# A streaming hybrid encoder step on one core: other bank counts, another pool order and a moved first-row block around the running streams' attention

## The chip, the cores and the metric

The kernel runs on one core of a Trainium2 chip. The core has a matrix engine (TensorE, PE in the profile, with its weight loads shown apart as PEld), a vector engine (DVE), a scalar engine (ACT), GpSimd (POOL) and a queue engine (SP) that issues nearly all transfers; 16 DMA engines carry them between the large memory (HBM) and the on-chip memory (SBUF). Matrix products land in PSUM, which has eight banks of 512 numbers of 32 bits for each of 128 partitions. The metric is the time of one launch in microseconds of device time; lower is better.

## The reference, cut to what matters

One layer of an encoder runs for two groups: one new stream of 1024 frames behind 16 meta rows (1040 rows) and eight running streams of 16 new frames each, with 272 cached rows of keys and values. Each row goes through a norm and one wide projection into queries, keys, values, the inputs of a state space scan and two gates. Attention (16 heads of 64) and the scan (32 heads of 64) run side by side and are merged through the gates; a causal convolution feed-forward net follows.

The attention is a stick-breaking one, with no softmax:

```python
def stick_breaking(q, k, v, q_pos, k_pos):
    z = jnp.einsum('bqhd,bshd->bhqs', q, k).astype(jnp.float32) * (SB_HEAD_DIM ** -0.5)
    reach = k_pos[None, :] < q_pos[:, None]
    log_beta = jax.nn.log_sigmoid(z)
    log_keep = jnp.where(reach, jax.nn.log_sigmoid(-z), 0.0)
    later = lax.cumsum(log_keep, axis=3, reverse=True) - log_keep
    w = jnp.where(reach, jnp.exp(log_beta + later), 0.0)
    return jnp.einsum('bhqs,bshd->bqhd', w.astype(v.dtype), v)
```

The kernel computes it without logarithms: beta = sigmoid(z), keep = 1 - beta, a running product of keep from the right, and weight = beta times the running product one place further right. In the merge the scan's output, normed over each of four groups, goes through `w_br_ssd` and is multiplied by its gate.

## The kernel before, in words

All 1168 rows (1040 + 128) are kept transposed in SBUF as `u`, split into a high and a low part, so that a 32-bit product is three matmuls in the faster form: high by high, high by low, low by high (`mm3`, lines 115, 118, 119). A projection block is 128 output columns: one weight load, split on ACT and DVE (lines 104 to 106), and three tiles of 384 to 400 rows, each 24 matmuls; 72 matmuls for a block.

The stages, in order: the norm; the scan (`phase_ssd`); the new stream's attention (`phase_att`); the running streams' attention (`phase_smp`); the merge (`phase_merge`); the feed-forward net (`phase_ffn`). Queries, keys and values go out to HBM (`s_qh`, `s_ql`, `s_kh`, `s_kl`, `s_v`) and are read back.

**The new stream's attention** goes over 8 pairs of heads. `head` (L684) loads KH, KL and QS (two buffers each), makes scores (L713, L716, PSUM tag `z`, two banks) for eight groups of 128 queries, each followed by `stick` (sigmoid on ACT, mask and complement on POOL, scan and product on DVE) into `beta0` to `beta7`, then transposes the weights (PSUM tag `wT`, two banks) and multiplies them by the values (PSUM tag `o`, two banks; L737, L738, L745). The groups begin at row 16; the first two query rows that are needed (rows 14 and 15) are done apart by `first_queries` (L752).

**The running streams' attention** (`sample_att`, L796) goes over 8 streams and 2 halves of the heads: 16 passes. Before them it loads the queries (`qhs`, `qls`), the new keys (`kxh`, `kxl`, 16 loads) and the last 16 cached key rows (`last`, 16 loads) and transposes these (PSUM tag `pk`). In a pass, 256 cached key rows are loaded (`ck`), transposed in two groups through `pk` and split into `Ksh` and `Ksl` (ACT copy, DVE subtraction); the queries are laid out on a diagonal (`qdh`, `qdl`, POOL); twelve matmuls make the scores (L873, L876, L877); sigmoid, mask, complement, scan and products give the weights; three transposes (`wT`) and a split follow; nine matmuls make the value product (L896 to L898, tag `o`); its result is copied to `od`, transposed back (`wT` again) and copied into `aout`, which is stored once at the end (L910).

**Filler.** Both stages alternate products with long chains on the other engines, so independent projection blocks are put between: 18 blocks of queries, keys and values and 16 gate blocks (`gate`, L659). `paced` (L960) draws a block when `done < len(marks) * rate` and ties each of its three tiles behind a marked matmul (`issue_after`): it may not be issued before it.

```python
    def paced(self, marks, done, rate):
        while self.fill and done < len(marks) * rate:
            at = lambda t: marks[min(int(t / rate), len(marks) - 1)]
            self.fill.pop(0)([at(done + t) for t in range(3)])
            done += 3
```

The new stream's attention has 64 marks and a rate of 1.17 and draws 25 of the 34 blocks. Of the other nine, `RESERVE` = 3 are held back for the start of the merge, and six go into the running streams' stage, at a rate of 3 x 6/16 tiles a pass; the mark of a pass is its first score matmul (L873).

**The merge.** `ssd_operands` (L925) makes 16 operands for `br_ssd`: for each it loads a block of the scan's output (`yt`, L933, two buffers), multiplies it by the row factors `rB` (L935, DVE), writes the high part (L936, ACT) and the low part (L937, DVE). The row factors come from `norm_rows` (L914) through HBM (`s_rs`). The second eight operands go into the slots of `u`. The held-back gate blocks stand ahead of `br_ssd` on PE.

**What sets the order.** Engines run their instructions in order, each with its own queue; SP issues the transfers in order too. A planner orders the instructions of each engine when the kernel is built, by estimated times, with earlier lines of the program first where two are ready. Each stage's pools are opened on top of the same base and closed again, so the next stage's tiles lie over the last stage's; a tile waits for the release of exactly those tiles that lay in its place. So the order in which a stage's pools are opened decides which old tile a new one has to wait for. The same holds for PSUM banks, in the order in which the tags are first used.

## Time and profile before

| what | us |
|---|---|
| median of 3 runs | 3043.59 (3042.37 to 3043.84) |
| profiled execution, its own time | 3041.27 |
| its span, first to last instruction | 3038.4 |
| PE busy in the span | 2936.0 |
| DVE, ACT, POOL busy | 1797.7, 1169.5, 600.3 |

The profiled execution is one run beside the three that were timed. The span leaves out some 2.9 us around the instructions. Shares of busy time are means over stages; the prediction reads the stages one by one. In the list of waits a line says who waited, for whom, how many us in total, how often, and the longest. In the list of instructions the bracket gives the idle time of the engine before the instruction and what ended it.

### The profile page before, as it was taken

The page shows a single profiled execution, that of the slowest core. Times are in us where ns is not written, and L with a number is a line of the kernel's source. Part 1 is how long each engine was busy: PE and PEld are TensorE (multiplying, and loading weights), DVE is VectorE, ACT ScalarE, POOL GpSimd, SP SyncE. Part 2 cuts the span into 40 slices and gives each one's busy share as a digit, 9 for nine tenths or more (in the row PEclk, how much of TensorE's full clock was granted, in tenths as well). Part 3 has the DMA queues.
Part 4 walks back from the last instruction along what each step waited for, and adds up shares of the span by engine and source line. Part 5 has one row for each costly group of instructions (what it writes and reads, how often), then busy time and mean ns, then how long its engine had stood idle before and what let it go on. Part 6 is the DMA issues. An engine that isn't in the chain of part 4 may idle for free.

```text
span 3038.4 us, 45425 instructions
## 1 busy us (share of the span) xinstructions
PE 2936.0 (97%) x17349; PEld 2792.5 (92%) x17349; DVE 1797.7 (59%) x2945; ACT 1169.5 (38%) x2294; POOL 600.3 (20%) x967
## 2 busy tenths in 40 slices
PE   7999999999999999999899899999999999999998
PEld 6998988979889999999799899999999999999997
DVE  6568677676666777777634441345755454545447
ACT  6432423324234554544444320214534242424245
POOL 0023132131232333333324000002201010101014
PEclk9999999999999999999899999999999999999999
DMA  5435355253474555544444553546211111111113
GB/s 187 110 95 150 97 141 151 76 157 104 133 215 130 165 153 143 155 124 110 84 122 149 158 180 97 149 109 190 73 46 44 43 44 43 43 43 38 41 43 118
DMA packets 445495, 338.43 MB, mean 111 GB/s; under 512 B 43991, under 2 KB 421155, under 8 KB 445279
## 3 DMA queue, kind: packets, MB, share of 16 engines
q1 hardware_dynamic: 445279, 335.54, 38.8%
q8 instruction: 136, 2.23, 0.3%
q14 instruction: 80, 0.66, 0.1%
HBM read 244.31 MB, written 91.15 MB: 110 GB/s over the span
## 4 chain that ended last, share of the span: by engine, by line
PE 43%; DVE 3%; DMA 2%; issue 1%; ACT 1%; POOL 0%; POOLq 0%; SPq 0%; ACTq 0%; DVEq 0%
PE mm L115 14%; PE mm L118 13%; PE mm L119 13%; DMA yt<-s_y 1%; DVE h L1192 1%; DVE sl L937 0%; DVE yt L935 0%; DVE wl L106 0%; PE o L896 0%; DMA ck<-in_cache_k 0%; PE tp L135 0%; PE o L898 0%; PE o L897 0%; DVE h L1170 0%; PE wT L135 0%
## 5 line engine op out<-in xcount | busy, mean ns | idle before, releaser
L115 PE MATMUL mm<-sh,wh 128*128 128x384 f32 (+3 forms) x2520 | 874.2, 347 | 13.3 <-ACT sh L936 5.1
L118 PE MATMUL mm<-sl,wh 128*128 128x384 f32 (+3 forms) x2520 | 870.5, 346 | 2.2 <-DVE sl L937 1.6
L119 PE MATMUL mm<-sh,wl 128*128 128x384 f32 (+3 forms) x2520 | 867.7, 345 | 0.0
L115 PEld LDWEIGHTS mm<-sh,wh 128*128 128x128 f32 (+1 forms) x2520 | 476.2, 189 | 28.0 <-issue 6.3
L118 PEld LDWEIGHTS mm<-sl,wh 128*128 128x128 f32 (+1 forms) x2520 | 476.6, 189 | 15.2 <-issue 9.2
L119 PEld LDWEIGHTS mm<-sh,wl 128*128 128x128 f32 (+1 forms) x2520 | 476.8, 189 | 8.9 <-issue 7.0
L115 PE MATMUL mm<-ph,wh 128*128 128x386 f32 x1248 | 424.3, 340 | 2.7 <-ACT ph L97 2.0
L118 PE MATMUL mm<-pl,wh 128*128 128x386 f32 x1248 | 424.7, 340 | 0.0
L119 PE MATMUL mm<-ph,wl 128*128 128x386 f32 x1248 | 422.4, 339 | 0.1
L106 DVE TENSOR_TENSOR wl<-wf,wh 128x1024 fp32r<-128x1024 f32 (+2 forms) x205 | 252.7, 1233 | 284.3 <-ACT wh L105 283.7
L105 ACT CAST wh<-wf 128x1024 fp32r<-128x1024 f32 (+2 forms) x205 | 212.5, 1037 | 485.1 <-PE mm L118 455.1
L1145 DVE SCALAR_TENSOR_TENSOR acc<-fx,cwf,acc 128x256 f32<-128x256 f32 (+1 forms) x352 | 170.8, 516 | 154.0 <-ACT acc L1143 150.1
L115 PEld LDWEIGHTS mm<-ph,wh 128*128 128x128 f32 x1248 | 236.2, 189 | 3.9 <-ACT ph L97 2.3
L119 PEld LDWEIGHTS mm<-ph,wl 128*128 128x128 f32 x1248 | 236.2, 189 | 0.9 <-DVE wl L106 0.5
L118 PEld LDWEIGHTS mm<-pl,wh 128*128 128x128 f32 x1248 | 235.2, 188 | 1.8
L680 DVE TENSOR_TENSOR_SCAN keep<-keep 128x144 f32<-128x144 f32 (+7 forms) x128 | 179.9, 1408 | 57.9 <-POOL keep L679 57.3
L115 PE MATMUL mm<-ah,wh 128*128 128x384 f32 x528 | 179.8, 340 | 0.0
L119 PE MATMUL mm<-ah,wl 128*128 128x384 f32 x528 | 179.2, 339 | 0.0
L118 PE MATMUL mm<-al,wh 128*128 128x384 f32 x528 | 178.6, 338 | 0.0
L1072 POOL TENSOR_TENSOR sq<-sq,sq 128x386 f32<-128x386 f32 (+1 forms) x42 | 60.2, 1433 | 467.1 <-ACT sq L1071 455.6
L98 DVE TENSOR_TENSOR wTl<-wT,wTh 128x512 fp32r<-128x512 f32 (+3 forms) x176 | 103.0, 602 | 80.6 <-ACT wTh L97 79.7
L1170 DVE TENSOR_TENSOR h<-mm,h 128x384 f32<-128x384 f32 x144 | 79.7, 555 | 119.8 <-PE mm L119 119.5
(326 smaller groups left out, 4535.2 us busy)
## 6 DMA issues: line engine op xcount, KB each, us to landing
wf<-in_w_in SPq DMA_DIRECT2D x80, 512.0 KB
wf<-in_w_up SPq DMA_DIRECT2D x44, 512.0 KB
t<-s_ac SPq DMA_DIRECT2D x36, 512.0 KB
wf<-in_w_down SPq DMA_DIRECT2D x28, 512.0 KB
wf<-in_w_out SPq DMA_DIRECT2D x24, 512.0 KB
s_y<-x SPq DMA_DIRECT2D x16, 577.0 KB
yt<-s_y SPq DMA_DIRECT2D x16, 577.0 KB
KH<-s_kh SPq DMA_DIRECT2D x32, 260.0 KB
```

The source lines that it names most:

```text
L98: nc.vector.tensor_tensor(out=l, in0=x, in1=h.bitcast(F32), op=ALU.subtract)
L105: nc.scalar.copy(wh, wf)
L106: nc.vector.tensor_tensor(out=wl, in0=wf, in1=wh.bitcast(F32), op=ALU.subtract)
L115: i = nc.tensor.matmul(p, wh[:, k, :], mh[:, c:c + w], start=s, stop=False)
L118: nc.tensor.matmul(p, wh[:, k, :], ml[:, c:c + w], start=False, stop=False)
L119: nc.tensor.matmul(p, wl[:, k, :], mh[:, c:c + w], start=False, stop=e)
L680: nc.vector.tensor_tensor_scan(out=K[:, ::-1], data0=K[:, ::-1], data1=K[:, ::-1], initial=1.0, op0=ALU.mult, op1=ALU.min)
L1072: nc.gpsimd.tensor_tensor(out=acc[:, :w], in0=acc[:, :w], in1=sq, op=ALU.add)
L1145: nc.vector.scalar_tensor_tensor(out=op, in0=src(q), scalar=w(q), in1=op, op0=ALU.mult, op1=ALU.add)
L1170: self.nc.vector.tensor_tensor(out=h, in0=p, in1=h, op=ALU.add)
L1192: nc.vector.tensor_scalar(out=h, in0=h, scalar1=self.gv[:, 24 + m:25 + m], scalar2=None, op0=ALU.mult)
```

## The change

- `first_queries` is called in the new stream's attention, ahead of the second head of the last pair, instead of at the start of the running streams' stage. Its tiles take the tags QS, KH and KL there, and its PSUM tiles that stage's `z` and `o`.
- In the running streams' stage `pk` has one bank instead of two and `o` two instead of one.
- The mark of a pass is its first value product (L896) instead of its first score matmul.
- `RESERVE` is 2 instead of 3: seven blocks go into the stage and two into the merge.
- The pools of both attention stages are opened in another order, and the fill stores' pool of the running streams' stage is opened last instead of first.
- `norm_rows` is called ahead of `sample_att` instead of behind it.

```diff
-RESERVE = 3
+RESERVE = 2
...
     def first_queries(self):
-        x = self.tile(ap, [128, 4, 288], F32R, 'Ksh').bitcast(F32).rearrange("p a b -> p (a b)")[:, :288]
+        x = self.tile(ap, [128, TP - T0], F32R, 'QS').bitcast(F32)[:, :288]
...
-        v = self.tile(ap, [128, 2, 512], F32R, 'Vsh').bitcast(F32)[:16].rearrange("p a (j c) -> p (a j) c", c=128)
+        v = self.tile(ap, [128, TP], F32R, 'KH').bitcast(F32)[:16, :1024].rearrange("p (j c) -> p j c", c=128)
...
-        Q = self.tile(ap, [128, 512], F32, 'last', bufs=2)[:, :256].rearrange("p (j c) -> p j c", c=32)
+        Q = self.tile(ap, [128, TP], F32R, 'KL').bitcast(F32)[:, :256].rearrange("p (j c) -> p j c", c=32)
...
-        ps = self.tile(pa, [128, 512], F32, 'z')
+        ps = self.tile(pa, [128, 512], F32, 'z', bufs=2)
...
-        po = self.tile(pa, [128, 512], F32, 'o')
+        po = self.tile(pa, [128, 512], F32, 'o', bufs=2)
...
     def sample_att(self, rate):
-            pk = self.tile(pa, [128, 512], F32, 'pk', bufs=2)
+            pk = self.tile(pa, [128, 512], F32, 'pk')
...
-                    pk = self.tile(pa, [128, 512], F32, 'pk', bufs=2)
+                    pk = self.tile(pa, [128, 512], F32, 'pk')
...
-                    mk = nc.tensor.matmul(z, qh, Kh[:, j], start=(j == 0), stop=False)
-                    if j == 0:
-                        marks.append(mk)
+                    nc.tensor.matmul(z, qh, Kh[:, j], start=(j == 0), stop=False)
...
-                po = self.tile(pa, [128, 512], F32, 'o')
+                po = self.tile(pa, [128, 512], F32, 'o', bufs=2)
...
-                    nc.tensor.matmul(po, wh[:, i], vh, start=(i == 0), stop=False)
+                    mk = nc.tensor.matmul(po, wh[:, i], vh, start=(i == 0), stop=False)
+                    if i == 0:
+                        marks.append(mk)
...
     def phase_att(self, right, rx):
-                'wTh', 'wTl', 'wf32', 'att', 'vf', 'KH', 'KL', 'QS', 'VV', 'keep', *(f'beta{i}' for i in range(8)))}
+                'KH', 'KL', 'QS', 'vf', 'keep', *(f'beta{i}' for i in range(8)), 'VV', 'wTh', 'wTl', 'wf32', 'att', 'fb', 'fw', 'fo')}
...
                 for e in range(2):
+                    if p == 7 and e == 1:
+                        self.first_queries()
                     marks += self.head(2 * p + e, v[:, :, 64 * e:64 * e + 64])
...
     def phase_smp(self):
-            mp = self.stp = self.pool(c2, "mixst", 3)
...
-                'aout', 'od', 'wTh', 'wTl', 'keep', 'beta', 'v', 'r', 'newton', 'qdh0', 'qhs', 'qls', 'kxh', 'kxl',
-                'last', 'V3h', 'V3l', 'qdl0', 'qdh1', 'qdl1', 'Ksh', 'Ksl', 'Vsh', 'Vsl',
-                'w30', 'w31', 'fb', 'fw', 'fo')}
+                'last', 'qhs', 'qls', 'kxh', 'kxl', 'qdh0', 'qdl0', 'qdh1', 'qdl1', 'Ksh', 'Ksl', 'V3h', 'V3l', 'v', 'r', 'newton',
+                'beta', 'keep', 'Vsh', 'Vsl', 'w30', 'w31', 'wTh', 'wTl', 'od', 'aout')}
+            self.stp = self.pool(c2, "mixst", 3)
...
-            self.first_queries()
+            self.norm_rows(self.ap)
             self.sample_att(3 * len(self.fill) / 16)
-            self.norm_rows(self.ap)
```

## The prediction, made before the changed kernel was run

> **What bounds the kernel now.** I read the page's shares first, then busy time by stretch from the last head's tail to the gated branch, then TensorE's (PE) waits in those stretches, then single instructions.
>
> ```profile
> PE 2936.0 (97%) x17349; PEld 2792.5 (92%) x17349; DVE 1797.7 (59%) x2945; ACT 1169.5 (38%) x2294; POOL 600.3 (20%) x967
> ```
> ```profile
> 1485.00:1522.00 37.00, 21.76 (x118) 17.03 (x117) 18.93 (x34) 14.47 (x32) 11.67 (x23) 0.74 0.74 127
> 1522.00:1678.00 156.00, 149.70 (x908) 142.36 (x908) 62.56 (x108) 66.03 (x132) 52.63 (x126) 0.98 0.43 136
> 1678.00:1700.00 22.00, 17.06 (x96) 13.30 (x95) 9.53 (x15) 12.48 (x24) 4.35 (x6) 1.00 0.28 82
> 1700.00:1738.00 38.00, 38.00 (x218) 38.00 (x217) 18.66 (x14) 12.42 (x17) 0.00 (x0) 1.00 0.67 192
> 1738.00:1788.00 50.00, 43.24 (x228) 41.71 (x227) 30.69 (x23) 16.19 (x15) 0.00 (x0) 0.93 0.70 219
> ```
>
> Columns after the stretch: PE, weight load, VectorE, ScalarE, GpSimd busy us (instructions), PE clock, DMA share, GB/s. PE is the bound nearly everywhere, so this change can win only where PE stands: the handover (1485 to 1522: 15.2 us idle), the streams' stage (1522 to 1700: 11.2) and the wait for the branch's operands (1738 to 1788). 218 matmuls in 38 us give 0.174 us each when PE never waits; a filler block, 72 of them, costs 12.6 us. By that price the 228 matmuls of 1738 to 1788 are 39.7 us of work, so 10.3 us are lost there. Some 37 us can be won in all.
>
> ```profile
> PE wT L135 <- DVE fb L783: 5.1, 1, 5.1
> ...
> PE pk L135 <- DMA last<-in_cache_k: 2.6, 1, 2.6
> ```
> ```profile
> PE wT L135 <- ACT od L900: 3.4, 3, 1.7
> ...
> PE z L873 <- ACT Ksh L97: 2.0, 4, 0.8
> PE z L876 <- DVE Ksl L98: 1.0, 2, 0.8
> ```
>
> Two waits of the handover, then three of the stage (us, times, longest). The largest is the first rows' own chain (fb).
>
> **The change part by part.**
>
> *First rows moved out, pools in order of release.* Before, the handover goes so:
>
> ```profile
> 1504.09 0.49 PE L135 MATMUL wT<-ident,beta 128*128 128x128 f32 x3
> ```
> ```profile
> 1505.05 0.64 PE L745 MATMUL o<-wf,VV 128*128 128x144 f32 x4 [0.22 <-ACT wf L743]
> 1505.62 0.68 PE L773 MATMUL z<-Ksh,last 128*32 128x16 f32 x16
> ...
> 1514.57 0.20 PE L135 MATMUL wT<-ident,fb 32*16 32x32 f32 x1 [5.08 <-DVE fb L783]
> 1515.04 3.62 PE L790 MATMUL o<-fw,Vsh 16*128 16x32 f32 x16 [0.26 <-ACT fw L787]
> ...
> 1521.95 0.53 PE L115 MATMUL mm<-sh,wh 128*128 128x384 f32 x1
> ```
> ```profile
> 1511.80 0.37 SPq L802 DMA_DIRECT2D qhs<-s_qh  x1
> 1522.00:1527.00 5.00, 5.00 (x18) 5.00 (x18) 1.54 (x5) 1.05 (x3) 0.94 (x2) 0.53 0.36 83
> ```
>
> The last head ends at 1505.7; the first filler matmul comes at 1521.95. Between lie the first rows, and loads that had to wait: counting tile sizes upward from the pools' common base, `qhs` lies over the last head's `att` tile, and `pk` over its `wT` banks. In the new order `last`, `qhs`, `qls` lie over the fill stores, `kxh`, `kxl` over rows and KH/KL (last read by the last head's scores), and the single `pk` bank over one of that head's score banks. So key rows, queries and the first cache transposes can go into the last head's tail. What still holds: `beta` lies over the last head's beta5 and beta6, read by transposes until about 1504 (first row). From there the first score chain runs with no filler:
>
> ```profile
> L879 ACT ACTIVATE beta<-z 128x288 f32<-128x288 f32 x16 | 6.6, 412 | 13.0 <-PE z L877 5.0 <-DVE beta L887 3.2 <-PE wT L135 2.2
> L882 POOL TENSOR_SCALAR keep<-beta 128x288 f32<-128x288 f32 x16 | 7.3, 458 | 1.0
> L883 DVE TENSOR_TENSOR_SCAN keep<-keep 128x288 f32<-128x288 f32 x16 | 13.1, 824 | 12.5 <-POOL keep L882 12.4
> L887 DVE TENSOR_TENSOR beta<-beta,keep 128x256 f32<-128x256 f32 x16 | 6.8, 427 | 0.0
> L97 ACT CAST wTh<-wT 128x384 fp32r<-128x384 f32 (+3 forms) x24 | 11.8, 494 | 9.1 <-PE wT L135 8.9
> ```
> ```profile
> 1511.58 1.28 ACT L919 ACT_TABLE_LOAD   x1 [4.83 <-DMA v<-s_ss]
> ```
>
> 0.41 + 0.46 + 0.82 + 0.43 + 0.49 = 2.6 us, with transposes, mask, small product and hand-offs some 5 us (estimate); the norm's square root, now ahead of the stage, may put its table load of 1.28 us in front of the sigmoid. First value product, and with it the first filler, at about 1511: 11 us earlier than 1521.95, and by then the first scores, key and weight transposes are done, about 2 us of work that before came later. At the clock of 0.53 the first 5 us of filler held 18 matmuls where 5/0.174 = 29 fit: 1.9 us lost, which a busier handover keeps. Together 15 us.
>
> The first rows' work isn't gone. At head 15 it costs PE 0.7 + 0.2 + 3.6 = 4.5 us (the rows above, some at low clock, so 3 to 4.5), where PE has no idle time to hide it. Its five loads and one store pass SP among gate stores and head loads; memset, two copies, mask and complement pass POOL, two products and a scan VectorE, which lie beside PE's filler. It takes over two-slot tags:
>
> ```profile
> 1420.38 0.44 SPq L692 DMA_DIRECT2D KH<-s_kh  x1
> ```
> ```profile
> 1457.70 0.28 PE L713 MATMUL z<-KH,QS 128*128 128x256 f32 x1
> ```
>
> Head 15's loads went out at 1420 and are read from 1457.7. Now the first rows take those slots; with a chain of some 20 to 25 us (loads at 1420, 10 us of chain as in 1505 to 1515, PE's queue) the slots are free at about 1445, and its loads (eight of some 260 KB, some 8 us, an estimate from their issue over 4 us) just fit. If not, what is late next is head 15's scores: head 14's slots are free at 1457, so at worst 8 us. Taken: 4.5 us, bounds 3 and 12. First term: 15 - 4.5 = 10.5 us won, bounds 2.5 and 12.
>
> The Trainium skill, "TensorE: Matmul & The Clock Gate", section "Part 1: The HAM clock gate", says the clock halves after an idle window of some 3.4 us. The trace agrees: after the 5.08 us wait it stands at 0.53. By that rule a handover with no such wait keeps the 1.9 us; if one stays, the sum is smaller by 1.9.
>
> *One bank for key transposes, two for value products, filler tied to these.* Each of 16 passes sends its keys through `pk` in two groups; each group is copied and subtracted:
>
> ```profile
> L98 DVE TENSOR_TENSOR Ksl<-pk,Ksh 128x512 fp32r<-128x512 f32 x32 | 21.4, 686 | 14.5 <-ACT Ksh L97 14.5
> L97 ACT CAST Ksh<-pk 128x512 fp32r<-128x512 f32 x32 | 18.3, 587 | 10.9 <-PE pk L135 8.8 <-issue 2.1
> ```
>
> With one bank the second group waits 0.59 + 0.69 = 1.27 us: 16 x 1.27 = 20 us if nothing covers it, 0 if the previous pass's value products and filler do. The two `o` banks can take away the `od` waits, 3.4 us, most of it in 1678 to 1700, where 22 us hold 17.06 of PE. Filler now starts after a pass's first value product instead of its first scores; it is drawn after passes 1, 3, 5, 7, 10, 12, 14 instead of 1, 3, 6, 9, 11, 14 (3 x 7 tiles over 16 passes instead of 3 x 6), so only the last pass ends quite bare, with the scores of both last passes mostly done. Of nine passes with no filler I charge half the 1.27 us, 5.7, and credit 3.4 of `od` and 2 of the tail: second term 0, bounds -20 and +6. Middle taken, because today's key waits (2.0 + 1.0 over 16 passes) are nearer to covered than to bare.
>
> *RESERVE 2.* Of nine gate blocks left, seven go into the stage and two into the merge; 12.6 us of work only change place. But the cover before the branch shrinks by as much.
>
> ```profile
> 1700.91 0.37 SPq L910 DMA_DIRECT2D s_att<-aout  x1
> 1706.57 0.81 SPq L933 DMA_DIRECT2D yt<-s_y  x2
> 1713.64 2.84 DVE L937 SCALAR_TENSOR_TENSOR sl<-yt,gv,sh 128x1154 fp32r<-128x1154 f32 x2
> 1784.38 2.83 DVE L937 SCALAR_TENSOR_TENSOR sl<-yt,gv,sh 128x1154 fp32r<-128x1154 f32 x2
> ```
> ```profile
> L854 POOL CAST Ksh<-kxh x16: 285/288/647, 1515.8 to 1664.0; 128x128 fp32r<-128x128 f32 x16
> ```
>
> `yt` waits for the last store of `aout`, over which it lies; the first operand is made at 1713.6, 13.5 us after the stage, the sixteenth by 1787. In the new order `rB` and `yt` lie over `last`, `qhs`, `qls`, `kxh`, last read (`kxh`) at 1664, 36 us before the end; two operands can be scaled within the stage, and the first low part waits only for `V3l`, which the last value products read. So the first operand stands when the stage ends: lead 13.5 us against 12.6 us less cover, third term +1, bounds -12 (no lead) and +7 (operands hardly the limit, of 10.3 lost). Moving the norm ahead costs nothing and brings nothing: its result was stored at 1537 already.
>
> ```profile
> 1537.00 0.45 SPq L923 DMA_DIRECT2D s_rs<-r  x1
> ```
>
> *Attention pools reordered.* KH, KL and QS now lie over the scan's constants and first buffers; head 0's loads go out 30 us before its first scores, so 0, bounds -3 and +1.
>
> **Sum.** 10.5 + 0 + 1 = 11.5 us. The profiled execution took 3041.27 us, span 3038.4; it would become 3029.8, and the median of the runs, 2.3 us higher, 3043.6 - 11.5 = 3032.1.
>
> **Rivals.**
>
> *Slower: the one key bank holds the pipeline.* If the next pass's keys aren't split before the value products run, its scores wait, and since filler is only let go by those products, nothing covers the chain of 2.6 us plus 1.27 us. Beside it lie the value products (nine of 512 columns, some 2 us), which leaves 1.9 us a pass: 30 us, giving 3032.1 + 30 = 3062. It decides (beyond 0.2% slower) from 18 us, 1.1 us a pass. For it: in 1678 to 1700, without filler, PE stands 5 us in some four passes, 1.2 us each. Against: key transposes are issued up to two passes ahead now. The Trainium skill, "PSUM — Partial Sum Buffer", section "PSUM bank collisions raise a hardware error", has it that no two engines may use one bank at once, which is why copy, subtraction and next transposes must take turns; no run here shows a collision.
>
> *No change to speak of: handover won, but lost again.* The first rows stall heads 14 and 15 (8 us more) or the operands get no lead (12.6 us): 3032.1 + 8 to 12.6 = 3040 to 3045. For it: every slot head 15 had free goes to the first rows. Against: the 30 us and more between load and use.
>
> *More won.* If `od` and key waits both vanish and the operands keep up, 10.5 + 6 + 7 = 23.5: 3020.1.
>
> **How the numbers follow.** My forecast, 3022 to 3037: 0.55; more won, below 3022: 0.13; no change to speak of, 3037.5 to 3049: 0.17; the key bank, slower: 0.15. 0.2% is 6 us, about what a measurement of this kernel can tell from no change. Faster 0.68, same 0.17, slower 0.15. The range 3017 to 3049 leaves out 0.05 below and 0.13 above; the forecast's own is 3022 to 3037.
>
> **What would show it.** Right: no fb chain between the last head and the first pass; first filler near 1511 (plus what the first rows add to the heads); no `yt` wait on `aout`, the first low part of an operand within 3 us of the last pass; `od` waits under 1 us. Wrong: waits of keys (Ksh, Ksl) over 10 us in the stage, a stall of head 15's scores on KH, or more than 12 us lost before the branch.

## The result, and the profile after

| | before | changed |
|---|---|---|
| median of the runs, us | 3043.72 (3042.37 to 3046.59) | 3073.53 (3069.69 to 3076.08) |
| ratio | | 1.0097, interval 1.0085 to 1.0109 |
| profiled execution: own time, span | 3041.27, 3038.4 | 3076.08, 3074.4 |

The change costs 0.97%, about 29.5 us; the forecast was 11.5 us won. The two profiled executions are 35 us apart in time and 36 in span, more than the medians, since the one of before lies just under its timed runs and the other is the longest of its four.

The shares of the page say little: PE is busy 20 us longer with the same 17349 matmuls.

```profile
PE 2955.7 (96%) x17349; PEld 2798.1 (91%) x17349; DVE 1797.1 (58%) x2945; ACT 1170.3 (38%) x2294; POOL 598.0 (19%) x967
```

The busy time by stretch, in the columns that the prediction used (PE, weight load, VectorE, ScalarE, GpSimd busy us, PE clock, DMA share, GB/s). These are the handover (two rows), the streams' stage, its tail, and the start of the branch:

```profile
1500.00:1520.00 20.00, 14.24 (x71) 10.56 (x69) 10.11 (x12) 7.04 (x14) 5.45 (x15) 0.82 0.82 129
1520.00:1545.00 25.00, 6.61 (x26) 5.07 (x27) 10.14 (x21) 9.73 (x18) 4.15 (x6) 0.58 0.43 121
1545.00:1740.00 195.00, 183.26 (x1029) 163.07 (x1028) 68.42 (x113) 71.94 (x146) 55.45 (x128) 0.98 0.39 122
1740.00:1755.00 15.00, 11.33 (x45) 8.41 (x46) 3.42 (x7) 6.17 (x13) 0.65 (x2) 0.77 0.19 55
1755.00:1830.00 75.00, 72.42 (x406) 70.89 (x405) 45.96 (x35) 25.68 (x26) 0.00 (x0) 1.00 0.66 208
```

Two things stand out. From 1520 to 1545 PE works 6.6 of 25 us: the handover got longer, not shorter. And 1755 to 1830, the start of the branch, is nearly full: that part came out better than forecast. The waits from the last head's end (1519.4) to the first filler matmul (1552.8), and then PE's own instructions there (start, duration, idle time before and what ended it):

```profile
PE pk L135 <- DVE kxl L98: 15.2, 2, 11.1
PE pk L135 <- DMA last<-in_cache_k: 2.8, 1, 2.8
PE z L873 <- ACT Ksh L97: 1.5, 2, 0.8
```
```profile
1522.39 0.63 PE L135 MATMUL pk<-ident,last 128*128 128x128 f32 x4 [2.76 <-DMA last<-in_cache_k]
1534.13 1.09 PE L135 MATMUL pk<-ident,last 128*128 128x128 f32 x4 [11.11 <-DVE kxl L98]
1539.28 1.09 PE L135 MATMUL pk<-ident,ck 128*128 128x128 f32 x4 [4.07 <-DVE kxl L98]
1541.14 0.58 PE L873 MATMUL z<-Ksh,qdh 128*128 128x288 f32 x1 [0.77 <-ACT Ksh L97]
1552.81 0.34 PE L115 MATMUL mm<-sh,wh 128*128 128x384 f32 x1
```

The fb chain is gone, but PE now stands at the transposes through the one `pk` bank: the second group of last rows can't be transposed until the first has been split (11.11 us), and the first cached keys until the second has (4.07 us). Not all of that is the bank's: with two banks (below) the first scores still come 16.7 us after the last head's end, against 21.7 here. The first scores come at 1541.1, the first value product and with it the first filler 11.7 us later. What the split itself waited for stands on ACT:

```profile
1525.00 1.28 ACT L919 ACT_TABLE_LOAD   x1 [6.06 <-DMA v<-s_ss]
1529.17 0.27 ACT L97 CAST kxh<-pk 128x128 fp32r<-128x128 f32 x1
```

and behind which transfers the last rows stood, on SP:

```profile
1501.38 0.37 SPq L807 DMA_DIRECT2D kxh<-s_kh  x1
1517.02 5.66 SPq L813 DMA_DIRECT2D last<-in_cache_k  x12
1522.79 0.47 SPq L918 DMA_DIRECT2D v<-s_ss  x1
```

Head 15, in whose slots the first rows now work:

```profile
1460.68 0.47 SPq L692 DMA_DIRECT2D KH<-s_kh  x1
```
```profile
1470.79 0.58 PE L713 MATMUL z<-KH,QS 128*128 128x256 f32 x1 [1.83 <-DMA QS<-s_ql]
1489.97 0.19 PE L135 MATMUL wT<-ident,fb 32*16 32x32 f32 x1
1494.34 1.97 PE L790 MATMUL o<-fw,KH 16*128 16x32 f32 x16
```

Its six loads go out from 1460.7 instead of 1418.3 (the prediction's row at 1420.38 is the third of them), when head 14's slots come free, because the first rows hold theirs until 1496; its scores begin at 1470.8 instead of 1457.7.

From trace to trace, the 36 us are: 14.0 until the last head's end (1505.4 to 1519.4; 3.8 of it stand already at the attention's first store of `att`, 946.9 to 950.7, and the other 10 come behind that), 16.9 from there to the first filler matmul (16.5 to 33.4), 22.2 from there to the last pass's end (178.8 to 201.0), less 17.1 behind it. The seventh block moves 12.6 from the last to the third, so the stage itself lost 9.6 and the branch won 4.5. The 3.8 can't be put down to the change: in the runs below that change nothing ahead of that store it comes anywhere from 948.9 to 953.2, later than in the trace of before.

### The profile page after: what moved, and what is told of

The parts are those of the page before. It is cut to its first block, busy times and chain, and to the rows that moved or that the text cites. A ratio compares the mean times of both kernels' runs of the same rounds, so it can differ in the third digit from the quotient of the medians.

```text
span 3074.4 us, 45439 instructions
## 1 busy us (share of the span) xinstructions
PE 2955.7 (96%) x17349; PEld 2798.1 (91%) x17349; DVE 1797.1 (58%) x2945; ACT 1170.3 (38%) x2294; POOL 598.0 (19%) x967
## 4 chain that ended last, share of the span: by engine, by line
PE 59%; DVE 4%; DMA 2%; ACT 2%; issue 2%; POOL 1%; SPq 1%; POOLq 0%; ACTq 0%; DVEq 0%
PE mm L115 17%; PE mm L118 17%; PE mm L119 17%; PE wT L135 2%; DMA yt<-s_y 1%; PE z L713 1%; PE z L716 1%; PE o L738 1%; PE o L737 1%; DVE wl L106 1%; DVE h L1193 1%; ACT wh L105 0%; DVE sl L937 0%; DVE yt L935 0%; PE o L135 0%
```

## The experiments

Two families: the changed kernel with one part taken back (names with a), and the kernel before with one part put in (names with b). Ratios are to the kernel before, 0.1% is 3.0 us. The first four were made to see whether the late handover, the key bank or the filler's mark carries the loss.

**Norm taken back.** `norm_rows` behind `sample_att` again:

```diff
-            self.norm_rows(self.ap)
             self.sample_att(3 * len(self.fill) / 16)
+            self.norm_rows(self.ap)
...
```

> The changed kernel with the norm of the scan's rows back behind the running streams' passes. Theory 1 (the handover is late because of what stands in order ahead of the key rows: late key-row loads behind the first rows' buffers, then the square root, for whose input ScalarE waited 6.1 us before it could split the key rows): the square root leaves the place ahead of the key split, 5 to 8 us less, near 3067. Theory 2 (the single key bank holds the pipeline, the rival of the prediction): no change, 3070 to 3076.

Measured: 3074.19, ratio 1.0094 (1.0077 to 1.0111). The first filler matmul comes at 1550.1 instead of 1552.8, and nothing is left of that at the end. With one bank, the square root that stands ahead of the split is not the cause; with two it was not tried.

**Banks taken back.** Two banks for `pk`, one for `o`:

```diff
...
-                    pk = self.tile(pa, [128, 512], F32, 'pk')
+                    pk = self.tile(pa, [128, 512], F32, 'pk', bufs=2)
...
-                po = self.tile(pa, [128, 512], F32, 'o', bufs=2)
+                po = self.tile(pa, [128, 512], F32, 'o')
```

> The changed kernel with two banks for key transposes and one for value products, as before. Theory 2 (the single key bank holds the pipeline): most of the 30 us come back, 3043 to 3053. Theory 1 (late key rows and the square root ahead of them): only the waits between two groups go, some 5 to 9 us in the handover and the stage together, 3064 to 3069, and the first filler stays later than 1540 us.

Measured: 3060.08, ratio 1.0047 (1.0032 to 1.0062): half of the loss, between the two theories. Nearly all of it is won in the stage: the first scores come at 1536.0, 5.2 us earlier, but the first filler matmul at 1550.7, only 2.1 us earlier; the last pass ends at 1734.9 instead of 1753.8.

**Mark taken back.** Filler tied to the first score matmul again:

```diff
-                    mk = nc.tensor.matmul(po, wh[:, i], vh, start=(i == 0), stop=False)
...
+                    mk = nc.tensor.matmul(z, qh, Kh[:, j], start=(j == 0), stop=False)
...
```

> The changed kernel with the filler tied to the first score matmul of a pass again. Theory 3 (the filler let go only by value products leaves the first passes bare): the first filler follows the first scores, 1541 instead of 1552.8 us, and 8 to 12 us come back, near 3064. Theories 1 and 2: the stage is held by the key rows either way, no more than 4 us, 3069 to 3075.

Measured: 3071.92, ratio 1.0087 (1.0072 to 1.0102). The first filler matmul comes 10.8 us earlier, at 1542.0, but the last pass ends only 3.6 us earlier. By this run alone the mark would be innocent; the square below shows that it isn't.

**First rows taken back.** `first_queries` at the start of the streams' stage, in its old tags:

```diff
-                    if p == 7 and e == 1:
-                        self.first_queries()
...
+            self.first_queries()
             self.norm_rows(self.ap)
...
```

> The changed kernel with the first rows back at the start of the running streams' stage, in that stage's tiles. Theory 1: head 15's loads go out at about 1423 again instead of 1461, the last head ends 10 us earlier, and the key rows come 10 to 15 us earlier; the first rows' own chain costs up to 9 us: 3060 to 3068. Theory 2: only the 10 us of head 15, less the chain's 9: 3068 to 3075.

Measured: 3071.09, ratio 1.0085 (1.007 to 1.01), as theory 2 had it. Head 15's loads go out at 1424.7 again, yet the last head ends at 1518.2, 1.2 us earlier only, and the first filler comes at 1549.3. All stores of `att` are 6 us later than in the trace of before from the first on (953.0, within the spread named above), and the last head loses another 6.7. A part of this is the first rows again, now on DVE: their addition stands in that queue ahead of the last head's weights and waits for its loads, and PE waits 2.98 us for those weights (`wTl`).

```profile
1510.44 0.31 DVE L762 TENSOR_TENSOR Ksh<-Ksh 128x144 f32<-128x144 f32 x1 [5.26 <-DMA Ksh<-s_kl]
```

**Attention's pools taken back.** The order of before in `phase_att`, `fb`, `fw`, `fo` at the end:

```diff
-                'KH', 'KL', 'QS', 'vf', 'keep', *(f'beta{i}' for i in range(8)), 'VV', 'wTh', 'wTl', 'wf32', 'att', 'fb', 'fw', 'fo')}
+                'wTh', 'wTl', 'wf32', 'att', 'vf', 'KH', 'KL', 'QS', 'VV', 'keep', *(f'beta{i}' for i in range(8)), 'fb', 'fw', 'fo')}
```

> The changed kernel with the attention's pools laid out in the order of before (wTh, wTl, wf32, att first; the first rows' fb, fw, fo at the end); all else as in the changed kernel. Theory A (the new order of the attention's pools costs by itself: KH, KL and QS come to lie over buffers that the scan reads last, so head 0's loads go out 8 us later): head 0's first KH load goes back from 890.4 to about 883 us, the first store of att to about 947, and the total falls by 3 to 6 us, to 3068 to 3071. Rival B (the head start's delay is paid by the scan's tail, whatever the order of pools, and the pools matter only in the handover, where last, qhs and qls now lie over wTh and wTl again): the stores of att stay late by 3.8 us, the handover gets longer by some us, the total 3073 to 3080.

Measured: 3074.98, ratio 1.0101 (1.0086 to 1.0116), as rival B had it. Head 0's loads go out 5 us earlier, at 885.3, and nothing is won: the last rows now go out early (1504.7 to 1516.2) and the key rows behind them only from 1521.7, so the first scores come at 1535.9 and the first filler at 1551.5.

Then the parts on the kernel before, one at a time.

**Banks alone** (the reverse of the diff above, and `o` with two banks in `first_queries` too):

> The kernel before with the banks alone exchanged: one bank for key transposes, two for value products. Theory A (the single key bank is slow by itself, as the run with two key banks and one value bank, 13.5 us faster than the changed kernel, says from the other side): 10 to 16 us slower than before, 3055 to 3061; the stretch from the first filler matmul to the last pass's end grows from 178 to about 190 us. Rival B (the single bank only hurts where filler is tied to value products, since scores' filler covers the turn between the two key groups): within 4 us of before, 3041 to 3049. Rival C (it hurts in the handover, where pass 0's key transposes stand behind the second group of transposed last rows): the first filler matmul comes 5 to 10 us later than 1521.95 and the stage itself keeps its 178 us.

Measured: 3057.17, ratio 1.0037 (1.0025 to 1.005). The stretch from the first filler to the last pass's end is 187.6 us against 178.8, the handover 23.2 against 16.5. So both theory A and rival C hold a share. A second profile of the same kernel:

> The kernel before with one key bank and two value banks once more, for a second profile of the same kernel: the stage's length from the first filler matmul to the last pass's end again 187 to 189 us.

It ran in 3058.57, and the stretch was 187.0 us.

**First rows alone** (into KH, KL, QS ahead of head 15):

> The kernel before with the first rows alone moved ahead of head 15, into the slots of KH, KL and QS, as the change does it. Theory A (their slot is held until their value products, at about 1496, so head 15's loads wait for head 14's slots, go out near 1457 and its scores slip by about 10 us; the handover loses the fb chain of some 9 us between the last head's end and the first pass): the last head's end moves from 1505.5 to about 1515, the first filler matmul comes 8 to 10 us after that, and the total is within 4 us of before, 3040 to 3047. Rival B (the move is a plain gain, and the changed kernel's loss comes from its other parts): 3033 to 3038. Rival C (the move is the main harm): 3053 or more.

Measured: 3045.59, ratio 1.0001 (0.9992 to 1.0011). Head 15 stalls as in the changed kernel:

```profile
1460.50 0.47 SPq L692 DMA_DIRECT2D KH<-s_kh  x1
```

The last head's end moves to 1516.6 (3.2 of the 11.2 us stand already at the first store of `att`), and from there to the last pass's end it takes 190.1 us instead of 195.3. What the move wins in the handover it loses at head 15; the two cancel.

**Streams' pools alone** (the changed kernel's order in `phase_smp`, `mixst` last):

> The kernel before with the streams' stage's pools alone laid out in the changed kernel's order (last, qhs, qls, kxh, kxl first, aout and mixst last; fb, fw, fo behind them). Theory A (the order gives the gated branch's operands their lead and costs nothing in the handover): the first low part of an operand comes 2 us after the last pass instead of 13, the total falls by 4 to 8 us, 3036 to 3040. Rival B (the lead comes, but in the handover tiles now wait for others of the last head than before, and the first filler matmul moves from 1521.95 to 1527 or later): 3042 to 3050.

Measured: 3051.08, ratio 1.002 (1.001 to 1.0029). The lead comes (first low part of an operand 1.6 us after the last pass), and it is paid for twice: from the first store of `att` to the last head's end it takes 563.5 us instead of 558.5, and the first filler comes 21.4 us after that end instead of 16.5. PE's waits from 1440 to 1545, then SP and ACT, tell how:

```profile
PE pk L135 <- DMA last<-in_cache_v: 11.9, 1, 11.9
PE wT L135 <- DVE beta L682: 3.7, 1, 3.7
PE o L737 <- ACT wTh L97: 3.4, 3, 2.7
```
```profile
1516.22 2.32 SPq L807 DMA_DIRECT2D kxh<-s_kh  x4
...
1529.62 3.76 SPq L813 DMA_DIRECT2D last<-in_cache_k  x8
```
```profile
1507.18 1.28 ACT L919 ACT_TABLE_LOAD   x1 [4.20 <-DMA v<-s_ss]
```

The key rows wait for their new slots until 1516.2, and the second half of the last rows stands behind them on SP until 1529.6. On ACT the square root waits for its rows while the last head's weights stand behind it (2.7 us). The list names cached values as the releaser of the 11.9 us; by the program's order the transposes that waited are those of the second group of last key rows (L813).

**RESERVE alone.**

> The kernel before with RESERVE at 2 alone: seven blocks in the streams' stage, two in front of the branch. Theory A (the block only changes its place, but the branch loses 12.6 us of cover while its first operand still comes 13 us after the last pass): the total is 5 to 12 us above before, 3049 to 3056. Rival B (the seventh block fills stage idle, which makes good what the branch loses): within 4 us of before, 3040 to 3048. Together with what the parts cost one by one so far (banks +12.8, the streams' pools +6.7, first rows +1.2, together 20.7 of 29.1) A would leave an interaction of about 0, B one of 8 us.

Measured: 3047.73, ratio 1.0016 (1.0006 to 1.0025), at the upper end of rival B's range, though the interval (2 to 8 us) reaches into theory A's: at least some of the cover lost ahead of the branch is made good in the stage.

**Mark alone, attention's pools alone:**

> The kernel before with the filler tied to the first value product of a pass instead of its first score matmul, and nothing else. Theory A (filler then comes after the first pass's whole chain, and the chain before it stands bare: the first filler matmul moves from 2 us after the first scores to their value product, some 20 us later, and only part of that is made up): 3 to 7 us slower, 3047 to 3051; with it the parts add up to the whole 29 us. Rival B (it costs 2 us as in the run on the changed kernel's side, and some 4 us of the whole are an interaction): 3045 to 3047.

> The kernel before with the attention's pools alone in the changed kernel's order. Theory A (as the run on the changed kernel's side says: head 0's loads go out some 5 us later and the stores of att some 2 to 4, but nothing is left of it at the end, or the handover makes it good): within 3 us of before. Rival B (the later start and a handover in which the streams' tiles lie over others cost 4 us or more, which the changed kernel's other waits cover): 3048 to 3054.

Measured: the mark 3054.6, ratio 1.0033 (1.0021 to 1.0045), which is more than either theory gave it; the pools 3046.74, ratio 1.0009 (1.0001 to 1.0018). With the mark the first filler comes at 1539.8, 31.0 us after the last head's end; PE has no filler for 14 us after its first scores (1525.9). With the pools the first filler comes 19.4 us after the last head's end (1507.1 to 1526.5), where PE now waits for the first rows' queries:

```profile
PE z L773 <- POOL last L770: 6.3, 1, 6.3
```

Head 0's loads go out later there too (888.9), but the first store of `att`, at 949.0, is not later than in other runs.

The parts on the kernel before add up to 1.16%, against 0.97% for the whole, while on the changed kernel the mark seemed to carry 0.1% and the bank 0.5%. So the square of banks by mark was filled on both sides.

> The kernel before with both: one key bank with two value banks, and filler tied to the first value product. Theory A (bank and mark bill the same time: with filler let go only after the value product, the turn of the one key bank falls into time in which TensorE stands anyway): less than their sum of 22.4, some 13 to 18 us above before, 3058 to 3063. Rival B (they add up, and the overlap of some 5 us lies elsewhere, in the handover): 20 to 25 us above, 3065 to 3070. Rival C (they make each other worse): 3072 or more.

> The changed kernel with both taken back: two key banks with one value bank, filler tied to the first scores. What is left is the two pool orders, RESERVE, the first rows and the norm, by the parts on the kernel before 12.3 us. Theory A (the two bill the same time, so that taking both back saves as much as the bank alone with a little more, 14 to 17 us): 3057 to 3060. Rival B (the mark saves its 9.9 us once the bank is back): 3048 to 3053.

| ratio to before | neither | key bank | mark | both |
|---|---|---|---|---|
| rest as before | 1 | 1.0037 | 1.0033 | 1.0067 (1.0054 to 1.008) |
| rest as changed | 0.9998 (0.9989 to 1.0007) | 1.0087 | 1.0047 | 1.0097 |

This shows where the loss is. With banks and mark taken back the changed kernel runs in 3045.96, the time of before and below what either theory gave it: the pool orders, the first rows, RESERVE and the norm together cost nothing that can be measured. Banks and mark cost 0.67% on the kernel before (3067.57), where they nearly add up (rival B), and 0.99% on the changed one, where they bill some of the same time: taking back both brings more than the two brought singly. There the key bank alone is worse than on the kernel before (1.0087 against 1.0037); for the mark (1.0047 against 1.0033) the intervals overlap. The remaining 0.3% appears only with both sides together. Likewise the other parts, 0.46% when each is put into the kernel before alone, come to nothing together; which of them makes good which was not taken apart.

The stretches from the last head's end to the first filler matmul, and from there to the last pass's end: first the kernel before, then the changed kernel, then the changed kernel with both taken back.

```profile
1505.40:1521.95 16.55, 7.66 (x50) 6.73 (x49) 5.12 (x17) 6.35 (x16) 7.08 (x15) 0.63 0.57 146
1521.95:1700.70 178.75, 167.51 (x1007) 156.41 (x1007) 72.14 (x123) 78.73 (x158) 56.98 (x132) 0.99 0.41 129
```
```profile
1519.40:1552.81 33.41, 13.83 (x61) 11.38 (x60) 13.36 (x27) 12.42 (x24) 6.89 (x17) 0.59 0.44 128
1552.81:1753.80 200.99, 186.40 (x1035) 164.10 (x1034) 68.62 (x113) 74.25 (x151) 53.37 (x120) 0.98 0.38 116
```
```profile
1517.60:1534.37 16.77, 4.68 (x21) 3.58 (x20) 7.95 (x18) 6.78 (x15) 4.04 (x6) 0.55 0.35 85
1534.37:1725.20 190.83, 180.62 (x1075) 169.44 (x1075) 75.03 (x123) 80.35 (x159) 55.54 (x130) 0.98 0.44 138
```

The last two kernels run the same 1096 matmuls there, in 234.4 and 207.6 us: 26.8 us for banks and mark, 16.6 in the handover and 10.2 in the stage. In the handover the first scores come 21.7 us after the last head's end instead of 16.4, and the first filler 11.7 us after them instead of 0.4. Of the 26.8, PE shows 14.9 as busy (200.2 against 185.3) and only 11.9 as idle. That is why the stage's list of waits looks harmless in the changed kernel:

```profile
PE o L894 <- ACT wTh L97: 2.8, 9, 0.6
PE wT L135 <- DVE beta L885: 2.8, 5, 2.1
PE pk L135 <- DVE Ksl L98: 2.1, 6, 0.8
PE z L874 <- DVE Ksl L98: 2.0, 6, 0.3
PE z L873 <- ACT Ksh L97: 1.2, 5, 0.3
...
PE wT L135 <- ACT od L900: 0.7, 1, 0.7
```

Part of a loss by alternation hides in busy time. At full clock (1.00 from 1575 to 1580) in the changed kernel:

```profile
1576.86 0.40 PE L874 MATMUL z<-Ksl,qdh 128*128 128x288 f32 x1 [0.33 <-DVE Ksl L98]
1577.10 0.29 PE L875 MATMUL z<-Ksh,qdl 128*128 128x288 f32 x1
1577.23 0.29 PE L873 MATMUL z<-Ksh,qdh 128*128 128x288 f32 x1
```

Behind the gap a score matmul is billed 0.40 us and the next begins 0.24 after it; in the stream they overlap and begin 0.13 us apart. The clock has the smaller share: the means of 0.59 over 33.4 us and 0.55 over 16.8 leave 13.7 and 7.5 us of full clock ungranted in the handovers, and the stages are alike at 0.98, so some 6 of the 14.9 us at most (an estimate from these means). Why the single bank costs more on the changed kernel's side (17.4 us in the stage and 4.8 in the handover, between the run with the mark taken back and the one with both) than on the kernel before (8.9 and 6.6) was not tested.

**Could the parts be had without the harm?** The first rows and the norm were put ahead of head 14, in buffers of their own that are free by then, so that no slot of KH, KL or QS is held:

```diff
...
+                        fr = c1.enter_context(ExitStack())
+                        self.fq = self.pool(fr, "first", 1, side='right')
...
+                    if p == 7 and e == 0:
+                        self.norm_rows(self.fq)
+                        self.first_queries()
                     marks += self.head(...)
...
```

> The kernel before with the first rows and the norm's square root put ahead of head 14, in buffers of their own on the free right side (released before the cache buffers are opened there), so that no slot of KH, KL or QS is held by them. Theory A (what the changed kernel's move lost at head 15 was the slots, 8 to 10 us of slipped scores; the handover's gain, no fb chain and no square root ahead of the key rows' split, is real): the last head's end stays within 5 us of 1505.5, the first filler matmul comes 10 to 13 us after it instead of 16.5, the total falls by 3 to 9 us, 3035 to 3041. Rival B (the handover is set by the transfers of the key rows and last rows, not by fb or the square root, and the first rows cost their 3 us on TensorE): 3043 to 3048.

Measured: 3039.05, ratio 0.9985 (0.9975 to 0.9994). The total falls as theory A said, but not by its steps: the last head's end moves by 7.8 us, to 1513.2 (5.3 of them stand already at the first store of `att`), and the first filler comes 15.4 us after it, hardly less than 16.5; the gain appears by the last pass's end, 188.0 us after the last head's instead of 195.3. What holds the handover now:

```profile
1515.68 1.09 PE L135 MATMUL pk<-ident,last 128*128 128x128 f32 x4 [2.21 <-DMA last<-in_cache_k]
1519.38 1.09 PE L135 MATMUL pk<-ident,last 128*128 128x128 f32 x4 [2.61 <-DMA last<-in_cache_k]
```

Then V3h in the place of aout, and wTh in that of od, so that the branch's first `yt` tiles lie over tiles that come free earlier:

```diff
-                'aout', 'od', 'wTh', 'wTl', 'keep', 'beta', ...
-                'last', 'V3h', 'V3l', ...
+                'V3h', 'wTh', 'od', 'wTl', 'keep', 'beta', ...
+                'last', 'aout', 'V3l', ...
```

> The same, and in the streams' pools V3h changes places with aout and wTh with od, so that the gated branch's first two yt tiles lie over V3h, wTh and od and not over aout. Theory A (the operands' lead is to be had without moving any tile that the handover needs): the first low part of an operand comes 3 to 7 us after the last pass instead of 13, the total is 4 to 6 us below that of the kernel without the exchange. Rival B (the operands are then limited by their rate, two yt buffers and 4.5 us a piece, and the lead is spent by the eighth): less than 2 us below it.

> The kernel with first rows and norm ahead of head 14 and V3h in aout's place once more, beside the one above: 3036 to 3039, 5 to 8 us below before.

Measured: 3037.53, ratio 0.9977 (0.9967 to 0.9988), and again 3038.01, 0.9976 (0.9967 to 0.9985). That is the best kernel of this study, some 7 us below before. The exchange alone is not shown to bring anything: the interval overlaps that of the run without it, and the first operand comes 10 us after the last pass (1699.3) instead of 13.6, not 3 to 7. Its `yt` loads do go out at once (1699.99); what follows takes its time:

```profile
1709.41 2.92 DVE L937 SCALAR_TENSOR_TENSOR sl<-yt,gv,sh 128x1154 fp32r<-128x1154 f32 x2
```

Last, the 16 loads of last rows ahead of the 16 of key rows, in that kernel:

> The kernel with first rows and norm ahead of head 14 and V3h in aout's place, and besides the 16 loads of last rows issued ahead of the 16 loads of key rows. Theory A (the handover is set by the last rows, which stand 14 us behind the key rows on SP: their transposes wait 2.0 and 2.7 us for them and the second group's split follows): the last rows are there before the last head ends, the first scores come 6 to 9 us after its end instead of 13.7, total 3 to 6 us below that kernel. Rival B (the slots of last are free only near 1500, so all loads behind them on SP wait and the key rows come later by as much): no gain, or 2 to 5 us slower.

Measured: 3040.12, ratio 0.9982 (0.9974 to 0.9991): no gain. The waits for last rows are gone, both groups are transposed at 1512.9, and another wait is in their place:

```profile
1512.86 1.07 PE L135 MATMUL pk<-ident,last 128*128 128x128 f32 x8
1517.75 1.94 PE L135 MATMUL pk<-ident,ck 128*128 128x128 f32 x8 [3.82 <-DVE kxl L98]
...
1526.44 0.61 PE L876 MATMUL z<-Ksh,qdh 128*128 128x288 f32 x1 [5.09 <-POOL qdh L860]
```

The first scores now wait for their queries on the diagonal. Rival B had the time, but neither theory had named that wait: the first scores need last rows, key rows and queries, and pulling one of the three forward only shows the next.

## Why the prediction was wrong, step by step

Two terms of the sum failed. The second, banks and mark, was put at 0 and carries the loss. The first, handover and head 15, was put at 10.5 us won and brought nothing: with banks and mark taken back, the parts that the forecast had at 11.5 us won run in 0.9998 of before, and their handover takes 16.8 us against 16.5.

**Handover, "together 15 us" won.** This step failed in three places. First, "key rows, queries and the first cache transposes can go into the last head's tail": I had counted over which tiles the key rows lie, but not when those come free, and the queues are in order. The key rows waited at the head of SP for the last scores of head 15, which came at 1501.2 instead of 1486.7 because the first rows held that head's buffers. Among SP's own waits from 1480 to 1535:

```profile
SPq L807 <- PE z L716: 4.4, 1, 4.4
```

So the key rows went out from 1501.4 instead of 1487.7 and the last rows behind them at 1517.0, and with one bank the cache transposes stood behind both groups of last rows. I costed the single bank in the passes only, and never in the handover. With two banks and the old mark PE still waits there, 6.5 us for last rows and 5.6 for the split of the keys, in the place of the fb chain. Second, "first value product, and with it the first filler", some 5 us after the first scores' start of chain: it took 11.7 us from the first scores to it, in a stretch whose clock was 0.59. Third, the square root: I named its table load and still wrote that it "costs nothing"; ACT stood 6.06 us for its rows. But taking it back brought nothing (1.0094), so here the words were wrong and the number, zero, stands. The 1.9 us of clock were not kept either: a wait of 11.11 us stayed, and the clock from 1520 to 1545 was 0.58. In all, where the first filler should have come 11 us earlier, it came 16.9 us later after the last head's end.

The Trainium skill, "DMA: Bandwidth & Descriptors", section "Anatomy of one DMA — SWDGE (gpsimd) path", notes, there of GpSimd's path, that a transfer's wait for a semaphore happens on the issuing sequencer, before dispatch. This case agrees: the second half of the last rows, issued at 1529.6 in the kernel with the streams' pools alone, stood behind key rows that waited until 1516.2.

**Head 15, "taken: 4.5 us, bounds 3 and 12".** The condition I wrote down came true ("if not, what is late next is head 15's scores: head 14's slots are free at 1457"): loads at 1460.7. I had a chain of 20 to 25 us; it ran from 1422 to 1496, because PE reached the small transpose only at 1490.0 (and the head has six loads, not eight; and 15 less 12 is 3, not the 2.5 of the term's lower bound). The scores slipped by 13.1 us, 3.8 of them already there by the later start. First rows alone, though, cost 1.0001: won and lost again, as the second rival had it for this part.

**Bank, banks, mark: "second term 0, bounds -20 and +6".** This is the term that carries the loss. Its size was wrong, not the list of mechanisms: both together cost 20.4 us (1.0067), the lower bound itself, on the kernel before, and 30 us (from 1.0097 to 0.9998) on the changed one. I took the middle because I read today's key waits as "nearer to covered than to bare". Those waits were small because of the second bank and of filler that started with the scores, and the change removes exactly these two: today's row was no measure of the covered share. The `od` waits did go (0.7 us), as said, but what they brought is inside the loss.

**RESERVE and the lead, "+1, bounds -12 and +7".** Right in mechanism and direction: the first low part of an operand comes 1.5 us after the last pass, as the test asked, and the branch won 4.5 us beyond the block that moved.

```profile
1755.29 1.42 DVE L937 SCALAR_TENSOR_TENSOR sl<-yt,gv,sh 128x1154 fp32r<-128x1154 f32 x1 [6.85 <-ACT sh L936]
```

RESERVE without the lead cost 0.16%, about 5 us, where the lower bound had 12. The lead's price was paid elsewhere, in the handover of the same pool order.

**Attention's pools, "0, bounds -3 and +1".** 0.09% (0.01% to 0.18%), about 3 us: the bound itself. Head 0's loads went out later, which I had not foreseen, but no loss by that shows in the first store of `att`; what the trace shows is a handover longer by 2.9 us, which I had not looked at for this part.

**The rivals.** The slower one, the key bank with filler let go only by value products, was the right mechanism: it named both halves, and with both taken back the whole loss is gone. Its price, 30 us, is what the two cost on the changed kernel, though more than half of that fell in the handover and not evenly on the passes; its time, 3062, came 11.5 us short because it still counted the forecast's gain as won. So the price came out right in part by luck. Its chance of 0.15 rested on the same reading of the key waits as the middle of the second term. The sign "waits of keys (Ksh, Ksl) over 10 us in the stage" did not show, though the rival came true (2.1, 2.0 and 1.2 us of key waits in the stage): the loss was in longer busy time and in the handover's 15.2 us behind `kxl`. The other wrong sign, a stall of head 15's scores on its loads, did.

## What to carry to other kernels

A resource that a change takes away (a bank, a cover) can't be priced by today's waits, because they are small on account of it; price it as if bare, and ask in which stretch it is bare first, which here was the start of the stage. Where tiles are laid over others in a new order, follow each transfer and each conversion in its own queue, not only to its slot: what waits at the head of SP or ACT holds all that stands behind it. And undo the parts in pairs as well as singly; taken back one at a time, the mark looked innocent here (0.1%), and with the bank it was half of the loss.

## What the runs showed of the hardware

A chain in pieces spreads a loss over busy time: the same 1096 matmuls of handover and stage showed 14.9 us more of busy time in the changed kernel than with banks and mark taken back, of which the granted clock (0.59 over 33.4 us against 0.55 over 16.8 in the handovers, 0.98 in both stages) can account for some 6 at most. SP issues the small loads of last rows at some 0.47 us each (12 in 5.66 us) and the key rows at some 0.6 (0.62 and 0.59 in the median), and what stands behind them in the queue waits for all of them: the 16 key rows, with some other transfers between, kept SP from 1501.4 to 1517.0 before the first of the last rows went out.
